# One core's decoder block: memory pools, instruction order and residual sums rearranged at four places

## Chip, cores and metric

One core of one Trainium2 chip. The metric is device microseconds of one execution; of several executions the median counts. The kernel before has run three times: 1854.45 us median, 1844.84 to 1854.69.

## The reference, cut to what matters

One layer of a decoder block on 512 tokens of width 1024, all in fp32. Every sub-block adds to the residual stream `x`:

```
x = x + hybrid_mixer(rmsnorm(x))            # DeltaNet and mLSTM heads, then mixed @ w_out
x = x + memory_cross_attention(rmsnorm(x), rmsnorm(mem))   # 256 memory tokens, 4 heads
x = x + peer_ffn(rmsnorm(x))                # 8 heads, each its 16 best of 128*128 experts
return rmsnorm(x)
```

In `peer_ffn` each token has per head two lists of 16 best keys; the sums of their values are the candidates, the 16 best candidates name the experts. With u and v the experts' rows of two tables of 16384 x 1024, the output of a token is the sum over its 128 experts of gate * gelu(u . h) * v.

## The kernel before

The 512 tokens are four tiles of 128. The mixer and cross attention work on the tiles in order. The experts are computed in two ways at once. Tiles 2 and 3 (DENSE, group G1) go over all experts: the dense loop (`peer_dense`) streams both tables in 128 blocks e of 128 experts, PE multiplies block e + 47 with the tokens ("pa", L1017), ACT applies Gelu (`act_`, L970), DVE multiplies by the gates, 8 blocks at a time (`gated`, L995; the gates come from DRAM through `gates_of` on POOL's queue), and PE adds block e to the outputs in PSUM (`add`, L998). In the last 47 blocks only `add` is left. Tiles 0 and 1 (G0) fetch the rows that each token needs: `peer_gather` issues from POOL one indirect DMA per expert slot (a "row": 128 tokens x 1024 values, 512 KB), 128 rows of u and then 128 rows of v for each tile, in the order u of tile 0, u of tile 1, v of tile 0, v of tile 1. DVE reduces a u row against the tokens (L1098) and accumulates a v row (L1109). Between them come Gelu on ACT (L1078) and the product with the gates (`weights_`). `close` adds the residual, loaded back from the output tensor, normalises, and stores.

`peer_gather` is a generator. A string, ORDER_XA, sets the order of cross attention and of what follows, and where rows are taken there ("p4" takes four): 158 of 512. In the dense loop 3.15 rows per block are taken, 2.3 in the last 47 blocks (L1035); what is left follows the loop (L1038). Then come the dense tiles' end (L1042 to L1065): residual and gains are loaded, the last block's products are added, DVE adds the residual out of PSUM into SBUF, ACT squares and sums, DVE scales, SP stores.

What is written is not the order in which an engine works. The framework orders each engine's instructions at build time, by the written order as priority and by its own estimate of when operands are ready; `keep_in_program_order` ties an instruction behind the one written before it on its engine. Each engine then takes its instructions strictly in order. Memory of a closed pool can be taken by a later pool, whose instructions wait until all instructions on the old pool's tiles are done.

At the seam between mixer and cross attention: the mixer's pools "mxp" and "mxw" hold its working tiles, and "mxp" also hT, the transposed activations, first of the input and then of the mixed heads. With hT the output projection is computed (`residual(..., "wout")`, L690 to L692; matmuls at L271, sums at L700), for tiles 0 and 1 first. When the mixer's `with` is left, pool "late" opens on the same memory. It holds all tiles of cross attention: gains (`row_(1, ...)`, L709, on POOL's queue), normalised tokens (W0), split weights (W2) and the transposed tokens of the two groups (dh0, dh1). `norm` (ACT squares, DVE scales, PE transposes at L209) and `query` (matmuls at L284) follow. Weights come through SP's queue into "w" and "wl", are copied to the leading part by ACT, and the rest is subtracted on POOL (L221) or DVE (L223).

`route_` of class Peer builds the candidates: per call seven additions on POOL (L844), on up to 8 heads x 16 values, then the 16 best on DVE. It is called five times (tile 0 in two halves), 35 additions.

Of the kernel before, what the change touches and what calls it, by code (L numbers as in the profile page):

```python
# [6 lines left out]
F32 = mybir.dt.float32  # L7
# [5 lines left out]
OP = mybir.AluOpType  # L13
# [62 lines left out]
def _body(ctx, tc, A, out, dbg):  # L76
# [137 lines left out]
    def hbuf(ph, n, name="hT"):  # L214
        t = ph.tile([P, 2, DB, n * P], F32R, name=name, bufs=1)
        return {"h": t[:, 0], "l": t[:, 1]}
# [380 lines left out]

    def mixer(tiles, aside):
        nt = len(tiles)
        with tc.tile_pool(name="mxp", bufs=nt) as ph, tc.tile_pool(name="mxw", bufs=2) as wk:  # L600
            ph = Phase(ph, tiles)
            hs = hbuf(ph, nt)
            mixed = {}
            steps = aside(wk)
            wr = wpool.tile([P, D], F32, name="wh")
# [78 lines left out]
            nc.sync.dma_start(x, A["x"].rearrange("(a p) d -> p a d", p=P))  # L684
            for ti in range(NT):
                X[ti] = x[:, ti]
            hs = hbuf(ph, nt)
            for i, ti in enumerate(tiles):
                transposed(mixed[ti].rearrange("p a b -> p (a b)"), hs, i)
            low_on[:] = [V]  # L690
            for k in range(0, nt, 2):
                residual(tiles[k:k + 2], {z: t[:, :, k * P:(k + 2) * P] for z, t in hs.items()}, "wout")  # L692
            for ti in tiles:
                tap(f"x1_{ti}", X[ti])

    def residual(tiles, hs, w):
        def ev(nb, i, ps):
            x = X[tiles[i]]
            c = slice(nb * 512, nb * 512 + 512)
            V.tensor_tensor(x[:, c], ps, x[:, c], op=OP.add)  # L700
        proj(hs, len(tiles), A[w], range(2), ev)
# [82 lines left out]
    class Peer:  # L784
# [50 lines left out]
        def route_(self, i, spot, hs, PH):  # L835
# [5 lines left out]
            off = 0  # L841
            for a0, n, w in RECT:
                o = cand[:, :, off:off + n * w].rearrange("p h (a b) -> p h a b", a=n)
                G.tensor_tensor(o, tvv[:, :, 0, a0:a0 + n].unsqueeze(3).to_broadcast([P, PH, n, w]),  # L844
                                tvv[:, :, 1, 0:w].unsqueeze(2).to_broadcast([P, PH, n, w]), op=OP.add)
                off += n * w
            yield
# [124 lines left out]
    def peer_dense(wu, psO, psC, rest):  # L972
# [40 lines left out]
        for e in range(NKEY):  # L1013
            n = e + AHEAD
            if n < NKEY:
                ps = psC.tile([P, 512], F32, name="pa")[:, :T]
                times(us.pop(0).rearrange("p (a b) -> p a b", a=DB), h, ps)  # L1017
            v = vs.pop(0)
            if e < NKEY - 1:
                for i in range(len(DENSE)):  # L1020
                    for z in range(2):
                        add(e, v, i, z)
            else:
                last.append((e, v))
            if n < NKEY:
                act_(n, ps)
            for g, at in gate_at.items():
                if at == e:
                    gated(g)
            for g, at in load_at.items():  # L1030
                if at == e:
                    gates_of(g)
            us.append(loaded_u(n + 2))
            vs.append(loaded_v(e + 2))
            steps += ROWS_BOTH if n < NKEY else ROWS_DOWN  # L1035
            run(rest, int(steps))
            steps -= int(steps)
        run(rest)  # L1038

        n = len(DENSE)  # L1040

# [7 lines left out]
        rs = []  # L1049
        for i, x in enumerate(xs):  # L1050
            for z, c in enumerate(half):
                for e, v in last:
                    add(e, v, i, z)
                V.tensor_tensor(x[:, c], outs[DENSE[i]][z], x[:, c], op=OP.add)
                SC.activation(junk[:, c], x[:, c], AF.Square, accum_out=ss[:, i, z:z + 1])
            if i:
                k = len(rs)
                t = sm.tile([P, n], F32, name="ft", bufs=1)
                V.tensor_tensor(t[:, k:i + 1], ss[:, k:i + 1, 0], ss[:, k:i + 1, 1], op=OP.add)
                r = rstd(t[:, k:i + 1], i + 1 - k, "n" if k == i else f"f{k}", 1.0 / D)  # L1060
                for j in range(k, i + 1):
                    rs.append(r[:, j - k:j - k + 1])
                    for c in half:
                        V.scalar_tensor_tensor(xs[j][:, c], xs[j][:, c], rs[j], w[:, c], op0=OP.mult, op1=OP.mult)
                        nc.sync.dma_start(out[DENSE[j] * P:(DENSE[j] + 1) * P, c], xs[j][:, c])  # L1065

    def peer_gather(ready, buffer):

        def fetch(table, ids, s):
            row = buffer()  # L1070
            G.indirect_dma_start(out=row, out_offset=None, in_=A[table],  # L1071
                                 in_offset=bass.IndirectOffsetOnAxis(ap=ids[:, s:s + 1], axis=0))
            return row
        late_, later = NSL // 2, NSL - 8

        def weights_(ti):

            SC.activation(act[ti], act[ti], AF.Gelu)  # L1078
            V.tensor_tensor(act[ti], act[ti], ready[ti], op=OP.mult)

        def close(ti):
            hn = first.hn[ti]
            x, wr, junk = buffer(), buffer(), buffer()
            G.dma_start(x, out[ti * P:(ti + 1) * P, :])
            row_(4, wr, G)
            V.tensor_tensor(hn, hn, x, op=OP.add)
            ss = sm.tile([P, 1], F32, name="nss")
            V.scalar_tensor_tensor(junk, hn, 1.0, hn, op0=OP.mult, op1=OP.mult, accum_out=ss)
            V.scalar_tensor_tensor(hn, hn, rstd(ss, 1, "n", 1.0 / D), wr, op0=OP.mult, op1=OP.mult)
            return out[ti * P:(ti + 1) * P, :], hn  # L1090

        act, done, stored = {}, [], []
        for ti in G0:
            act[ti] = per.tile([P, NSL], F32, name=f"act{ti}", bufs=1)
            hn, ids = first.hn[ti], first.ids[first.tiles.index(ti)].rearrange("p a b -> p (a b)")
# [7 lines left out]
        for ti in G0:  # L1103
            hn, ids = first.hn[ti], first.ids[first.tiles.index(ti)].rearrange("p a b -> p (a b)")
            for s in range(NSL):
                row = fetch("pv", ids, s)
                w = act[ti][:, s:s + 1]
                if s:
                    V.scalar_tensor_tensor(hn, row, w, hn, op0=OP.mult, op1=OP.add)  # L1109
                else:  # L1110
                    V.tensor_scalar(hn, row, w, None, op0=OP.mult)
                if s == later and ti == G0[0]:
                    weights_(done.pop())
                if s == late_ and ti != G0[0]:
                    stored.append(close(G0[0]))
                if s == late_ + 32 and stored:
                    G.dma_start(*stored.pop())
                yield
        G.dma_start(*close(G0[1]))

    mixer(tuple(range(NT)), memory_kv)
    mxs.close()
# [7 lines left out]

    def eight(t):
        return t[:, 0:2].rearrange("p a b -> p (a b)").rearrange("p (a b) -> p a b", a=DB)
    for i in range(2):
        t = late.tile([P, 2, DB, 2 * P], F32R, name=f"dh{i}")
        dh.append({"h": t[:, 0], "l": t[:, 1]})
    pe = ctx.enter_context(ExitStack())
    sct = pe.enter_context(tc.tile_pool(name="sct", bufs=1, side="right"))
# [57 lines left out]
    for what in ORDER_XA.split():  # L1195
# [3 lines left out]
        elif kind == "q":  # L1199
            n, x, y = (int(c) for c in what[1:])  # L1200
            query(GS[n], range(x, y))
            if n and y == DB:
                t = late.tile([P, 4, D], F32, name="dh1")
                dh[1] = {"f": eight(t), "room": t}
        elif kind == "s":
            soft_[n] = soft(n)
# [122 lines left out]
```

## Time and profile before

| | |
|---|---|
| median of three runs | 1854.45 us |
| profiled execution | 1853.35 us, span of its instructions 1851.6 us |
| busy PE / DVE / POOL / ACT | 90% / 69% / 45% / 22% of the span |
| moved by DMA | 519.02 MB, mean 280 GB/s |
| granted TensorE clock, mean | 0.957 of full speed |

The span runs from the first to the last instruction of the profiled execution; what lies around it is the difference to its time. Busy shares are averages over stages with different limits: up to about 490 us the mixer, to about 590 cross attention, then routing and gathers together, from about 1030 the dense loop beside the gathers, and from about 1820 the end. In a timeline a bracket names the idle time of the engine before the instruction and what ended it. PE's matmuls in fp32 stand as two records each.

### The profile page before, as it was taken

What the parts mean: (1) busy time and instruction counts of PE and PEld (TensorE: products, weight loads), DVE (VectorE), ACT (ScalarE), POOL (GpSimd) and SP (SyncE); (2) the same over time, 40 slices, a digit from 0 to 9 for tenths busy, and PEclk for the clock granted to TensorE, in tenths of its full rate; (3) what the DMA queues carried; (4) which work ended last, traced back from release to release, by engine and by line L of the source; (5) the groups of instructions that cost most, each with busy time, mean ns of one, the idle gap of its engine ahead of it and who ended that gap; (6) DMA issues with size and microseconds to landing.
All of it is one profiled execution on the core that took longest, in us unless ns stands there. A gap on an engine that the chain in (4) does not pass through costs nothing.

```text
span 1851.6 us, 21460 instructions
## 1 busy us (share of the span) xinstructions
PE 1671.7 (90%) x7468; PEld 1233.1 (67%) x7468; DVE 1269.1 (69%) x2789; ACT 406.2 (22%) x786; POOL 842.2 (45%) x685
## 2 busy tenths in 40 slices
PE   5999999999799976996999879993999999999993
PEld 3878788776598853885888656662666666664441
DVE  6656654665633698999998875557666566566668
ACT  5433532554353131211223110000000000000000
POOL 2121111331123054556354566566666666666663
PEclk9999999999899988998999979997999999999997
DMA  4211211235535477999899999999999999999996
GB/s 139 63 49 43 69 40 46 69 103 193 182 125 171 143 267 276 345 350 347 289 340 395 367 402 410 410 410 409 410 410 410 409 409 410 410 409 409 409 410 253
DMA packets 166508, 519.02 MB, mean 280 GB/s; under 512 B 15744, under 2 KB 44544, under 8 KB 164608
## 3 DMA queue, kind: packets, MB, share of 16 engines
q0 software_dynamic: 76752, 286.82, 39.6%
q1 hardware_dynamic: 60720, 216.15, 31.8%
q10 hardware_dynamic: 28928, 14.68, 2.7%
q8 instruction: 59, 0.97, 0.2%
q14 instruction: 49, 0.40, 0.1%
HBM read 498.71 MB, written 18.87 MB: 280 GB/s over the span
## 4 chain that ended last, share of the span: by engine, by line
DMA 36%; PE 33%; DVE 17%; issue 8%; POOL 4%; ACT 2%; ACTq 1%; SPq 0%; DVEq 0%; POOLq 0%
DMA row<-in_pv,ids 8%; PE pj L313 8%; PE pj L284 7%; PE pj L271 5%; PE acc L445 4%; DMA wh<-in_pv,ids 4%; DMA Vm<-in_pv,ids 3%; DMA W<-gates__132 3%; PE acc L943 3%; DMA W<-in_pv,ids 3%; DMA row<-in_pu,ids 3%; DMA wl<-in_pv,ids 2%; DVE W L1098 2%; DMA wl<-in_pu,ids 2%; DMA KT<-in_pu,ids 2%
## 5 line engine op out<-in xcount | busy, mean ns | idle before, releaser
L998 PE MATMUL o<-ld,W 128*128 128x512 f32 x832 | 371.3, 596 | 4.5 <-DVE W L951 4.5
L313 PE MATMUL pa<-dh,ld 128*128 128x256 f32 x1296 | 295.7, 381 | 35.8 <-ACT dh L970 34.2
L313 PEld LDWEIGHTS pa<-dh,ld 128*128 128x128 f32 x1296 | 247.4, 191 | 104.1 <-issue 39.3
L998 PEld LDWEIGHTS o<-ld,W 128*128 128x128 f32 x832 | 158.9, 191 | 175.9 <-issue 167.5
L221 POOL TENSOR_TENSOR wl<-w,wh 128x1024 fp32r<-128x1024 f32 x32 | 76.9, 2408 | 307.6 <-ACT wh L236 265.8
L313 PE MATMUL pj<-dh,w 128*128 128x256 f32 x640 | 148.0, 387 | 0.2 <-ACT dh L294 0.2
L1071 POOL DMA_INDIRECT W<-in_pu,ids x73 | 95.0, 1302 | 92.1 <-DVE W L1098 53.6
L313 PEld LDWEIGHTS pj<-dh,w 128*128 128x128 f32 x640 | 122.6, 195 | 17.2 <-ACT dh L294 0.7
L1109 DVE SCALAR_TENSOR_TENSOR dh<-row,act,dh 128x1024 f32<-128x1024 f32 x72 | 92.5, 1284 | 57.1 <-DMA row<-in_pv,ids 56.8
L1071 POOL DMA_INDIRECT row<-in_pu,ids x74 | 97.6, 1319 | 60.9 <-issue 19.3
L1071 POOL DMA_INDIRECT row<-in_pv,ids x74 | 99.4, 1343 | 51.3 <-issue 17.4
L970 ACT ACTIVATE W<-pa 128x256 f32<-128x256 f32 x65 | 24.9, 383 | 407.6 <-PE pa L313 397.5
L313 PE MATMUL pj<-dh 128*128 128x256 f32 x496 | 111.7, 379 | 0.0
L271 PE MATMUL pj<-wh,hT 128*128 128x512 f32 x320 | 108.5, 410 | 1.3 <-ACT wh L236 1.3
L284 PE MATMUL pj<-hT,wh 128*128 128x512 f32 x320 | 109.1, 414 | 0.0
L1098 DVE SCALAR_TENSOR_TENSOR row<-row,dh 128x1024 f32<-128x1024 f32 x74 | 88.4, 1222 | 22.5 <-DMA row<-in_pu,ids 22.1
L1098 DVE SCALAR_TENSOR_TENSOR W<-W,dh 128x1024 f32<-128x1024 f32 x73 | 88.5, 1220 | 19.2 <-DMA W<-in_pu,ids 19.2
L313 PEld LDWEIGHTS pj<-dh 128*128 128x128 f32 x496 | 93.5, 191 | 12.2
L236 ACT ACTIVATE wh<-w 128x1024 fp32r<-128x1024 f32 x64 | 67.7, 1058 | 106.8 <-DMA w<-in_wout 27.7
L998 PE MATMUL o<-ld,dh 128*128 128x512 f32 x192 | 85.2, 592 | 0.0
L1071 POOL DMA_INDIRECT wh<-in_pu,ids x40 | 56.6, 1415 | 51.2 <-DVE wh L1098 26.2
L1071 POOL DMA_INDIRECT wl<-in_pu,ids x41 | 54.6, 1332 | 47.8 <-PE pj L313 17.9
(432 smaller groups left out, 3143.5 us busy)
## 6 DMA issues: line engine op xcount, KB each, us to landing
ld<-in_pv SPq DMA_DIRECT2D x128, 512.0 KB, 6.8
ld<-in_pt SPq DMA_DIRECT2D x81, 512.0 KB, 6.9
gates__132<-W ACTq DMA_DIRECT2D x16, 896.0 KB, 16.4
W<-gates__132 POOLq DMA_DIRECT2D x14, 1024.0 KB, 17.4
w<-in_pt SPq DMA_DIRECT2D x24, 512.0 KB, 6.7
dh<-in_pt SPq DMA_DIRECT2D x23, 512.0 KB, 6.7
w<-in_win SPq DMA_DIRECT2D x20, 512.0 KB, 3.6
w<-in_wout SPq DMA_DIRECT2D x16, 512.0 KB, 3.7
```

The costliest lines, as they stand in the source:

```text
L221: G.tensor_tensor(out, a, hi, op=OP.subtract)
L236: SC.activation(hi, wt, AF.Copy)
L271: PE.matmul(acc[i], a[:, d, i * P:(i + 1) * P], b[:, z], start=d == 0 and m == 0, stop=d == DB - 1 and m == len(pairs) - 1)
L284: PE.matmul(acc[:, :n * P], a[:, d], b[:, d], start=d == 0 and m == 0, stop=d == DB - 1 and m == 2)
L313: PE.matmul(ps, w[:, d], h[:, d], start=d == 0, stop=d == DB - 1)
L445: PE.matmul(ps[:, i], l[:, i], r[:, i], start=True, stop=True)
L943: PE.matmul(ps[:, k], oj[:, a, :, k], og[:, g, a, :, k], start=g == 0, stop=g == 1)
L970: SC.activation(place(e), ps, AF.Gelu)
L998: PE.matmul(outs[DENSE[i]][z], place(e)[:, i * P:(i + 1) * P], v[:, z * 512:(z + 1) * 512], start=e == 0, stop=e == NKEY - 1)
L1071: G.indirect_dma_start(out=row, out_offset=None, in_=A[table], in_offset=bass.IndirectOffsetOnAxis(ap=ids[:, s:s + 1], axis=0))
L1098: V.scalar_tensor_tensor(row, row, 1.0, hn, op0=OP.mult, op1=OP.mult, accum_out=act[ti][:, s:s + 1])
L1109: V.scalar_tensor_tensor(hn, row, w, hn, op0=OP.mult, op1=OP.add)
```

## The change

- The mixer is cut in two. `mixed_tiles` does all up to the transposed mixed heads, with hT in a pool "mxh" of its own, and closes its working pools; `mixer` then computes the output projection. dh1 moves from "late" to a further pool "later".
- The candidates' additions go from POOL to VectorE.
- The Gelu on ACT between u and v rows is tied to its written place.
- Rows are counted (`taken`). The dense loop and the call behind it take all but the last 6 (TAIL) of 512; these follow the dense tiles' end, each tied to its written place on DVE, with the close of tile 1 and its store, which goes from POOL's queue to SP's.
- Dense tiles: PE adds the residual into PSUM by a product with the identity, and ACT and DVE read PSUM; DVE's four sums go. Gathered tiles: the residual is loaded with the first v row, which becomes a multiply-add on it, and the sum in `close` goes; the gains are loaded 8 rows ahead of `close`; scaling and store are done in halves.

```diff
     def mixer(tiles, aside):
         nt = len(tiles)
+        with tc.tile_pool(name="mxh", bufs=1) as hp:
+            hs = mixed_tiles(tiles, aside, hp)
+
+            low_on[:] = [V]
+            for k in range(0, nt, 2):
+                residual(tiles[k:k + 2], {z: t[:, :, k * P:(k + 2) * P] for z, t in hs.items()}, "wout")
...
+    def mixed_tiles(tiles, aside, hp):
+
+        nt = len(tiles)
         with tc.tile_pool(name="mxp", bufs=nt) as ph, tc.tile_pool(name="mxw", bufs=2) as wk:
             ph = Phase(ph, tiles)
-            hs = hbuf(ph, nt)
+            hs = hbuf(hp, nt)
...
-            hs = hbuf(ph, nt)
+            hs = hbuf(hp, nt)
             for i, ti in enumerate(tiles):
                 transposed(mixed[ti].rearrange("p a b -> p (a b)"), hs, i)
-            low_on[:] = [V]
-            for k in range(0, nt, 2):
-                residual(tiles[k:k + 2], {z: t[:, :, k * P:(k + 2) * P] for z, t in hs.items()}, "wout")
...
+            return hs
...
-                G.tensor_tensor(o, tvv[:, :, 0, a0:a0 + n].unsqueeze(3).to_broadcast([P, PH, n, w]),
+                V.tensor_tensor(o, tvv[:, :, 0, a0:a0 + n].unsqueeze(3).to_broadcast([P, PH, n, w]),
...
-            run(rest, int(steps))
+            run(rest, min(int(steps), 4 * NSL - TAIL - taken[0]))
             steps -= int(steps)
-        run(rest)
+        run(rest, 4 * NSL - TAIL - taken[0])
...
             for z, c in enumerate(half):
+                PE.matmul(outs[DENSE[i]][z], I, x[:, c], start=False, stop=False)
                 for e, v in last:
                     add(e, v, i, z)
-                V.tensor_tensor(x[:, c], outs[DENSE[i]][z], x[:, c], op=OP.add)
-                SC.activation(junk[:, c], x[:, c], AF.Square, accum_out=ss[:, i, z:z + 1])
+                SC.activation(junk[:, c], outs[DENSE[i]][z], AF.Square, accum_out=ss[:, i, z:z + 1])
...
-                    for c in half:
-                        V.scalar_tensor_tensor(xs[j][:, c], xs[j][:, c], rs[j], w[:, c], op0=OP.mult, op1=OP.mult)
+                    for z, c in enumerate(half):
+                        V.scalar_tensor_tensor(xs[j][:, c], outs[DENSE[j]][z], rs[j], w[:, c], op0=OP.mult, op1=OP.mult)
                         nc.sync.dma_start(out[DENSE[j] * P:(DENSE[j] + 1) * P, c], xs[j][:, c])
+        run(rest)
+        for to, half_ in stored:
+            nc.sync.dma_start(to, half_)
+
+    taken = [0]
+    TAIL = 6
+    stored = []
...
             row = buffer()
+            taken[0] += 1
...
-            SC.activation(act[ti], act[ti], AF.Gelu)
+            tc.keep_in_program_order(SC.activation(act[ti], act[ti], AF.Gelu))
...
-        def close(ti):
-            hn = first.hn[ti]
-            x, wr, junk = buffer(), buffer(), buffer()
+        def residual_(ti):
+            x = buffer()
             G.dma_start(x, out[ti * P:(ti + 1) * P, :])
-            row_(4, wr, G)
-            V.tensor_tensor(hn, hn, x, op=OP.add)
+            return x
+
+        def close(ti, wr):
+
+            hn, junk = first.hn[ti], buffer()
             ss = sm.tile([P, 1], F32, name="nss")
             V.scalar_tensor_tensor(junk, hn, 1.0, hn, op0=OP.mult, op1=OP.mult, accum_out=ss)
-            V.scalar_tensor_tensor(hn, hn, rstd(ss, 1, "n", 1.0 / D), wr, op0=OP.mult, op1=OP.mult)
-            return out[ti * P:(ti + 1) * P, :], hn
+            r = rstd(ss, 1, "n", 1.0 / D)
+            for c in (slice(0, 512), slice(512, D)):
+                V.scalar_tensor_tensor(hn[:, c], hn[:, c], r, wr[:, c], op0=OP.mult, op1=OP.mult)
+                stored.append((out[ti * P:(ti + 1) * P, c], hn[:, c]))
...
                 w = act[ti][:, s:s + 1]
-                if s:
-                    V.scalar_tensor_tensor(hn, row, w, hn, op0=OP.mult, op1=OP.add)
-                else:
-                    V.tensor_scalar(hn, row, w, None, op0=OP.mult)
+                done_ = V.scalar_tensor_tensor(hn, row, w, hn if s else residual_(ti), op0=OP.mult, op1=OP.add)
+                if taken[0] > 4 * NSL - TAIL:
+                    tc.keep_in_program_order(done_)
...
+                if s == late_ - 8 and ti != G0[0] or s == later and ti == G0[1]:
+                    wr = row_(4, buffer(), G)
                 if s == late_ and ti != G0[0]:
-                    stored.append(close(G0[0]))
+                    close(G0[0], wr)
                 if s == late_ + 32 and stored:
-                    G.dma_start(*stored.pop())
+                    for _ in range(2):
+                        G.dma_start(*stored.pop())
                 yield
-        G.dma_start(*close(G0[1]))
+        close(G0[1], wr)
...
+    lates = late, pool("later", 1, side="right")
     for i in range(2):
-        t = late.tile([P, 2, DB, 2 * P], F32R, name=f"dh{i}")
+        t = lates[i].tile([P, 2, DB, 2 * P], F32R, name=f"dh{i}")
```

## Rows read from the trace of the kernel before

**Rows 1.** Windows: stretch, length, busy PE, PEld, DVE, ACT, POOL, clock, DMA share, GB/s.

```profile
741.00:972.00 231.00, 215.58 (x1129) 191.28 (x1129) 224.81 (x703) 46.67 (x97) 124.32 (x98) 0.97 0.92 334
...
1111.00:1265.00 154.00, 154.00 (x534) 101.11 (x533) 89.84 (x137) 7.68 (x20) 95.71 (x70) 1.00 1.03 410
...
1265.00:1299.00 34.00, 0.08 (x1) 0.00 (x0) 29.38 (x46) 0.38 (x2) 24.32 (x24) 0.57 1.03 410
...
1825.00:1830.00 5.00, 0.00 (x0) 0.00 (x0) 4.86 (x5) 0.00 (x0) 0.00 (x0) 0.60 0.99 396
```

**Rows 2.** Timeline of PE, 487 to 503 us: start, duration, engine, line, what.

```profile
487.02 0.40 PE L271 MATMUL pj<-wh,hT 128*128 128x512 f32 x1
...
497.20 1.94 PE L209 MATMUL tr<-UI,W 128*128 128x128 f32 x8 [9.78 <-issue]
...
502.54 24.42 PE L284 MATMUL pj<-dh,W 128*128 128x256 f32 x192
```

**Rows 3.** Timeline of DVE, SP's queue and POOL around the same seam.

```profile
463.05 0.68 DVE L700 TENSOR_TENSOR x<-pj,x 128x512 f32<-128x512 f32 x1
...
482.00 2.89 SPq L246 DMA_DIRECT2D w<-in_wq  x2
...
487.74 0.74 POOL L191 DMA_DIRECT2D W<-in_nrow  x1 [59.46 <-PE pj L271]
...
490.68 2.34 POOL L221 TENSOR_TENSOR W<-w,W 128x1024 fp32r<-128x1024 f32 x1 [2.21 <-ACT W L251]
```

**Rows 4.** DMA issues, 480 to 500 us: count, KB each, us to landing.

```profile
w<-in_wq SPq DMA_DIRECT2D x4, 512.0 KB, 3.6
...
W<-in_nrow POOLq DMA_DIRECT2D x1, 512.0 KB, 8.1
```

**Rows 5.** Timeline of POOL and DVE, the candidates' additions and DVE's nearest operation.

```profile
673.64 1.17 POOL L844 TENSOR_TENSOR cand<-tv 128x32 f32<-128x32 f32 x6 [9.64 <-DVE tv L778]
...
838.09 0.23 DVE L859 TENSOR_TENSOR step<-key 128x120 f16<-128x120 f16 x1
...
838.22 0.21 DVE L781 MAX8 bv<-tk 128x8 f32<-128x50 f32 x1
...
838.25 6.80 POOL L844 TENSOR_TENSOR cand<-tv 128x128 f32<-128x128 f32 x7
...
869.24 1.23 DVE L1098 SCALAR_TENSOR_TENSOR row<-row,dh 128x1024 f32<-128x1024 f32 x1 [2.94 <-DMA row<-in_pu,ids]
```

**Rows 6.** Timeline of ACT and PE at the pause of 1265 us.

```profile
1298.62 0.31 ACT L1078 ACTIVATE act<-act 128x128 f32<-128x128 f32 x1 [50.33 <-DVE row L1098]
...
1299.26 5.91 PE L313 MATMUL pa<-dh,ld 128*128 128x256 f32 x16 [34.18 <-ACT dh L970]
```

**Rows 7.** Timeline of DVE and PE, the last 75 us.

```profile
1777.76 2.28 DVE L995 TENSOR_TENSOR dh<-dh,W 128x2048 f32<-128x2048 f32 x1
...
1793.55 27.63 PE L998 MATMUL o<-ld,dh 128*128 128x512 f32 x64
...
1808.42 1.28 DVE L1109 SCALAR_TENSOR_TENSOR dh<-row,act,dh 128x1024 f32<-128x1024 f32 x1 [0.32 <-DMA row<-in_pv,ids]
...
1833.51 1.22 DVE L1086 TENSOR_TENSOR dh<-dh,W 128x1024 f32<-128x1024 f32 x1
...
1834.77 1.22 DVE L1088 SCALAR_TENSOR_TENSOR KT<-dh 128x1024 f32<-128x1024 f32 x1
...
1836.04 0.15 DVE L174 TENSOR_SCALAR nv<-nss 128x1 f32<-128x1 f32 x1
...
1838.36 1.28 DVE L1089 SCALAR_TENSOR_TENSOR dh<-dh,nr,W 128x1024 f32<-128x1024 f32 x1
...
1839.56 2.48 DVE L1054 TENSOR_TENSOR ld<-o,ld 128x512 f32<-128x512 f32 x4
...
1842.91 0.16 DVE L1059 TENSOR_TENSOR ft<-fss 128x2 f32<-128x2 f32 x1 [0.88 <-ACT ld L1055]
...
1845.49 2.74 DVE L1064 SCALAR_TENSOR_TENSOR ld<-ld,f0r 128x512 f32<-128x512 f32 x4
```

More of the change, by code (lines that the diff above doesn't have):

```diff
@@ L599, in mixer @@
         nt = len(tiles)
+        with tc.tile_pool(name="mxh", bufs=1) as hp:
[3 more added lines that the diff above has]
+                residual(tiles[k:k + 2], {z: t[:, :, k * P:(k + 2) * P] for z, t in hs.items()}, "wout")
+            for ti in tiles:
+                tap(f"x1_{ti}", X[ti])
+    def mixed_tiles(tiles, aside, hp):
+        nt = len(tiles)
         with tc.tile_pool(name="mxp", bufs=nt) as ph, tc.tile_pool(name="mxw", bufs=2) as wk:
             ph = Phase(ph, tiles)
-            hs = hbuf(ph, nt)
+            hs = hbuf(hp, nt)
             mixed = {}
@@ L686, in mixer @@
                 X[ti] = x[:, ti]
-            hs = hbuf(ph, nt)
+            hs = hbuf(hp, nt)
             for i, ti in enumerate(tiles):
                 transposed(mixed[ti].rearrange("p a b -> p (a b)"), hs, i)
-            low_on[:] = [V]
-            for k in range(0, nt, 2):
-                residual(tiles[k:k + 2], {z: t[:, :, k * P:(k + 2) * P] for z, t in hs.items()}, "wout")
-            for ti in tiles:
-                tap(f"x1_{ti}", X[ti])
+            return hs
     def residual(tiles, hs, w):
@@ L1076, in weights_ @@
         def weights_(ti):
-            SC.activation(act[ti], act[ti], AF.Gelu)
+            tc.keep_in_program_order(SC.activation(act[ti], act[ti], AF.Gelu))
             V.tensor_tensor(act[ti], act[ti], ready[ti], op=OP.mult)
-        def close(ti):
-            hn = first.hn[ti]
-            x, wr, junk = buffer(), buffer(), buffer()
+        def residual_(ti):
+            x = buffer()
             G.dma_start(x, out[ti * P:(ti + 1) * P, :])
-            row_(4, wr, G)
-            V.tensor_tensor(hn, hn, x, op=OP.add)
+            return x
+        def close(ti, wr):
+            hn, junk = first.hn[ti], buffer()
             ss = sm.tile([P, 1], F32, name="nss")
             V.scalar_tensor_tensor(junk, hn, 1.0, hn, op0=OP.mult, op1=OP.mult, accum_out=ss)
-            V.scalar_tensor_tensor(hn, hn, rstd(ss, 1, "n", 1.0 / D), wr, op0=OP.mult, op1=OP.mult)
-            return out[ti * P:(ti + 1) * P, :], hn
-        act, done, stored = {}, [], []
+            r = rstd(ss, 1, "n", 1.0 / D)
+            for c in (slice(0, 512), slice(512, D)):
+                V.scalar_tensor_tensor(hn[:, c], hn[:, c], r, wr[:, c], op0=OP.mult, op1=OP.mult)
+                stored.append((out[ti * P:(ti + 1) * P, c], hn[:, c]))
+        act, done = {}, []
         for ti in G0:
@@ L1202, in _body @@
             if n and y == DB:
-                t = late.tile([P, 4, D], F32, name="dh1")
+                t = lates[1].tile([P, 4, D], F32, name="dh1")
                 dh[1] = {"f": eight(t), "room": t}
```

## The prediction, made before the changed kernel ran

> **What bounds the kernel now.** I read the windows by stage first, then the PE timeline at the seam between mixer and cross attention, then the waits, then the DVE timeline of the last 45 us. The windows [rows 1] show three regimes. From 741 to 972 us DVE is busy 224.8 of 231 us while the DMA engines move 334 GB/s: DVE sets the pace. From 1111 us on the DMA share is 1.03 and the rate stands at 410 GB/s, in the stretch where PE works all the time (1111 to 1265) and also in the one where PE does nothing (1265 to 1299); at 1825 it is still 396. So from 1111 at the latest to about 1827 the gathered rows and the streamed tables together fill the DMA engines, and PE is not what ends the stage. Behind that comes a tail on DVE alone. Ahead of all of it, at 487 us, PE stands still while memory changes hands [rows 2, 3].
>
> The profiled execution took 1853.35 us and its span 1851.6, so 1.75 us lie around the span. It is 1.1 us below the median of the three runs, 1854.45 (1844.84 to 1854.69). A difference of 0.5%, 9.3 us, is about what a measurement of this kernel can tell from none.
>
> **1. Cross attention beside the mixer's last product.** Now the last matmul of the output projection ends at 487.4 and the first query matmul starts at 502.54 [rows 2]. Between them lie the load of the norm's gains on POOL (L709), which waited for the last matmul, POOL standing for 59.46 us, and then landed after 8.1 us [rows 3, 4], the two norms, and 16 transposes. POOL waited since all tiles of pool "late" wait for the mixer's pool, which holds hT, the operand of that product. Afterwards hT lives in a pool of its own, and only "later" (dh1, which the second pair of tiles needs) shares its memory: the gains, the norm of tiles 0 and 1 and their transposes can run from 463.7, when these tiles' sums are finished [rows 3], beside PE's second half of the product. What then holds the queries? The weights' buffers come from the old rotation: the first load issues at 482.00 and lands 3.6 us later, at 485.6; copy and subtraction (2.21 and 2.34) put the last part at 490.2 at the latest, and the first two of three passes need less [rows 3, 4]. The transposes stay on PE, now inside the product: 16 cost at most 3.9 at the 1.94 for 8 of [rows 2], nothing where they fall into PE's waits for weights; I take 2, and the product ends at 489.4. The 512 KB of gains then load beside the product's weights: at most 1.3 us at 410 GB/s. So queries start near 490.5: **-12 us**. From there to about 650 PE is the chain, so all later work moves along. Ends: 0 (the seam stays) and -15.1 (the whole gap).
>
> **2. Candidates' sums on DVE.** 35 additions leave POOL, where they stand in front of gathers; the last seven held it 6.8 us [rows 5]. On DVE the nearest row, 120 elements of two inputs, lasts 0.23 and the next one starts 0.13 later: 35 of them are 4.6 to 8.1 us. DVE is full there, so this lies on the path; I take 4.9, since most of these tiles have 24 to 64 columns. Against it stands the 2.94 us that DVE waited at 869 for a row, whose issue stood behind those 6.8 us. Sum **+2 us**; ends +8.1 (nothing saved) and -7.7 (the 9.64 us for which POOL stood at the second seven come back as well). The Trainium skill, "Perfetto Trace Analysis", Identifying the Most-Contended Engine, says to relieve the engine with the highest occupancy, which speaks against this part. By it the whole 4.9 us would be lost and the sum be 1845.5; the trace agrees as to the engine, with 224.8 of 231 us.
>
> **3. The pinned Gelu.** ACT's Gelu of the second gathered tile's activations (L1078) stands too early in ACT's order: it waited 50.33 us for that tile's last product, the evictions of "pa" stood behind it, and PE stood 34.18 us [rows 6]. Pinned to its program place it comes at row 376 of 512; 158 rows are taken in the written order and 3.15 per block of the dense loop, so that is e = 69, and the products it waits for are 120 rows old. It waits for nothing. PE gets 34 us ahead. I cost this at nothing: while PE stood, the DMA engines moved 410 GB/s of gathered rows, and those rows are now moved later instead. The Trainium skill, "Perfetto Trace Analysis", Optimization Strategies, says to free what blocks the matmul engine when it idles; by that rule the 34 us come off. The trace disagrees as far as the rate goes. What is late next: gated(15) (L995) stands behind row 479 in DVE's order (33 rows follow it) and was done at 1780.0, 13.5 us before PE used its tiles at 1793.55 [rows 7]; with PE 34 us ahead PE waits there. A row is 512 KB, 1.28 us at 410 GB/s. At worst 27 rows (34.18 / 1.28) are consumed without streamed tables beside them, at DVE's 1.32: **+1.1 us**; ends 0 and 1.1.
>
> **4. The tail.** From 1808.42 DVE has 19 rows at 1.32 to 1833.51; then the residual 1.26, square 1.27, rstd 2.32, scaling 1.2, four sums 2.5, a wait of 0.88 for ACT, rstd 2.58, four scalings to 1848.23 [rows 7]: 39.8 us. Afterwards: the residual load and the gains come at rows 385 and 504, ahead of rows that they now delay by 2 x 1.28, so I count 21 rows, 27.7; dense rstd 2.6 and scalings 2.7 between rows 506 and 507; square 1.3, rstd 2.3, two half scalings 1.4: 38.0. That is **-1.8 us**; the last store lands as before. PE gets four identity matmuls, each two records of 0.43: 3.4 us, so PE ends at 1824.6 and ACT 0.8 later. DVE would arrive after row 506, at 1828, so this is covered by 2.6 us. If that cover is gone, DVE waits with six rows and the closing behind it. The first row of each tile becomes a multiply-add like the others and one 1.22 addition of the first tile goes, both under the DMA limit. On SP the last two half stores stand behind the four dense ones; on POOL the two residual loads and two gains' loads move ahead of gathers, at about the 0.74 of such a load in [rows 3], and the first tile's store becomes two: under 4 us of issue in a stage of some 700 that waits for the transfers.
>
> Sum: 1853.35 - 12 + 2 + 1.1 - 1.8 = **1842.6 us**, 0.64% below the median.
>
> **Rivals.** (a) PE's stall is the bound. The 34.18 us would come off too, and the 1.1 of part 3 with them: 1842.6 - 35.3 = 1807.3. For it: PE works without a pause around the stall [rows 1]. Against it: 410 GB/s through the stall. The rule of the Trainium skill that part 3 names leads here. 7%.
>
> (b) The gathers between 650 and 1080, where DVE's order is redrawn by the scheduler, fill the idle DMA time better: at 334 of 410 GB/s over 231 us there are 43 us of transfers to be had; a quarter gives 1832. 8%.
>
> (c) The overlap does not come: the norm waits for the seam after all, or the gain is lost before 1080. Then 1853.35 + 2 + 1.1 - 1.8 = 1854.6. For it: the order on each engine is the scheduler's, which may put the norms behind the product. Against it: nothing else held POOL at the seam than the product [rows 3]. 15%.
>
> (d) Slower: the six pinned rows wait for PE. Place: DVE's first instruction of the dense end. Behind gated(15) PE needs 2.3 + 27.6 + 3.4 and ACT 0.8, 34 us; DVE gets from row 479 to 506 in 35.6. From row 481 on, each row that gated(15) slips back costs 1.3 us; from row 497 on the change is slower; behind row 505 DVE waits 32 us with everything queued: 1842.6 + 32 = 1875. Against it: the Gelu at e = 69 holds back the scheduler's picture of the rows, which draws gated(15) forward. 8%.
>
> **How the numbers follow.** The forecast has 62%, with 1832 to 1852 as its own range (overlap -15 to -8, sums -4 to +8, order). Faster by over 0.5% means below 1845.2: 0.45 of the forecast's 0.62, (a) and (b): 0.60. Slower, above 1863.7: most of (d) and a little of (c): 0.08. The rest 0.32. The range 1826 to 1860 leaves out (a), most of (d) and the edges.
>
> **What would show it.** Right: the first query matmul near 490, the gains' load on POOL issued near 442 with no wait for the last product; no Gelu wait on ACT and no PE gap at 1265; the DMA rate at 410 GB/s until some 38 us before the end; 35 additions of 0.13 to 0.23 on DVE; and between rows 506 and 507 no wait. Wrong: a span that falls with the PE gap, a seam that stays, or a wait of DVE for ACT ahead of the dense scaling.

## The result, and the profile after

The changed kernel takes 1842.06 us (median of 15 runs, 1837.02 to 1845.13); the kernel before, run beside it, takes 1850.37 us (15 runs, 1844.83 to 1859.73). The ratio is 0.9946, with an interval of 0.9932 to 0.9960: by it 10.0 us (7.4 to 12.6) of 1850.4 are gone, by the two medians 8.3. The prediction of 1842.6 us holds in its value, and of its range, 1826 to 1860, little was needed. Three of its parts came out at about their size; the fourth, the candidates, cost 2.8 us alone and 3.7 to 5.9 in pairs of kernels, where +2 was put.

The profiled execution of the changed kernel took 1837.1 us (span 1835.3), 5 us less than its median; that of before took 1853.35 (span 1851.6), 3 more than its new median. So the two traces differ by 16.3 us where the medians differ by 8.3, and sizes of a few us are read from rounds of runs here, not from two traces.

First the windows, which answer [rows 1] (stretch, length, busy PE, PEld, DVE, ACT, POOL with counts, granted clock, DMA share, GB/s), of the changed kernel:

```profile
741.00:972.00 231.00, 222.69 (x1173) 197.69 (x1172) 222.10 (x697) 51.83 (x103) 114.59 (x82) 0.98 0.95 344
1111.00:1265.00 154.00, 154.00 (x539) 102.16 (x538) 89.07 (x140) 9.03 (x24) 93.99 (x72) 1.00 1.03 410
1265.00:1299.00 34.00, 34.00 (x121) 22.61 (x120) 20.15 (x30) 1.90 (x5) 19.50 (x17) 1.00 1.03 410
```

From 1265 to 1299 us PE is now busy for all 34.00 us, where it had been busy for 0.08; the DMA engines move 410 GB/s in both. The regimes are the same: VectorE full to about 972, the DMA engines full from 1111 at the latest.

Where the time went shows in the bytes. The same view over longer stretches, first of the kernel before:

```profile
0.00:460.00 460.00, 418.66 (x2332) 337.82 (x2333) 274.84 (x723) 207.53 (x379) 95.75 (x57) 0.98 0.25 81
460.00:650.00 190.00, 177.15 (x1012) 156.01 (x1011) 96.38 (x333) 71.44 (x123) 34.12 (x70) 0.96 0.48 155
650.00:1100.00 450.00, 388.90 (x1928) 320.17 (x1927) 408.63 (x1227) 95.22 (x199) 240.79 (x201) 0.92 0.92 337
...
1250.00:1700.00 450.00, 415.82 (x1395) 266.00 (x1394) 289.00 (x255) 20.78 (x55) 293.76 (x224) 0.96 1.03 410
```

and of the changed kernel:

```profile
0.00:460.00 460.00, 420.75 (x2349) 339.96 (x2350) 277.69 (x729) 210.09 (x383) 96.55 (x58) 0.99 0.26 83
460.00:650.00 190.00, 180.39 (x1041) 159.09 (x1041) 107.53 (x389) 71.30 (x131) 43.48 (x71) 0.99 0.54 177
650.00:1100.00 450.00, 401.30 (x1947) 328.20 (x1948) 407.49 (x1211) 94.19 (x190) 228.33 (x170) 0.93 0.94 340
...
1250.00:1700.00 450.00, 450.00 (x1456) 276.45 (x1455) 275.43 (x236) 20.17 (x53) 285.56 (x213) 1.00 1.03 410
```

Length times rate gives the megabytes. Up to 460 us the changed kernel is 0.9 MB ahead (38.2 against 37.3), from 460 to 650 it gains 4.2 (33.6 against 29.5), from 650 to 1100 another 1.4 (153.0 against 151.7). Together that is 6.4 MB, and at 410 GB/s 15.7 us: nearly the whole 16.3 us between the spans. The 0.9 MB ahead of the seam are scatter and not the change: by 460 us the fourteen traces of this document, those of the experiments among them, have moved 37.2 to 38.3 MB, with the old seam as with the new one. From 460 to 650 us the ten kernels with the new seam move 31.6 to 34.3 MB and the four with the old one 29.4 to 30.3, on the mean 3.2 MB apart, or 7.8 us. From 650 to 1100 the two kinds do not differ (150.1 to 153.1 and 149.8 to 154.5). After 1250 both move 410 GB/s, though PE works 34 us more in that stretch than before.

At the seam itself, which answers [rows 2, 3], the timeline of PE and POOL in the changed kernel:

```profile
436.61 0.74 POOL L191 DMA_DIRECT2D W<-in_nrow  x1 [12.90 <-PE tr L209]
...
464.83 0.71 PE L209 MATMUL tr<-UI,W 128*128 128x128 f32 x5
...
483.52 0.39 PE L271 MATMUL pj<-wh,hT 128*128 128x512 f32 x1
483.75 0.71 PE L209 MATMUL tr<-UI,W 128*128 128x128 f32 x5
485.20 0.38 PE L284 MATMUL pj<-dh,W 128*128 128x256 f32 x1 [0.74 <-ACT dh L211]
485.93 3.25 PE L284 MATMUL pj<-dh,W 128*128 128x256 f32 x25 [0.34 <-DVE dh L212]
491.06 20.17 PE L284 MATMUL pj<-dh,W 128*128 128x256 f32 x166 [1.88 <-DVE W L223]
```

The gains load at 436.6 with no wait for the last product. Eleven of the 16 transposes run inside the product from 464.8 on, the last five behind it, and the queries start at 485.20, where they had started at 502.54. What holds them next is the low part of the weights, 1.88 us, after which the other 166 records run on from 491.06.

The end, which answers [rows 7], from the timeline of DVE:

```profile
1712.67 2.28 DVE L1003 TENSOR_TENSOR dh<-dh,W 128x2048 f32<-128x2048 f32 x1
...
1812.46 1.28 DVE L1128 SCALAR_TENSOR_TENSOR dh<-row,act,dh 128x1024 f32<-128x1024 f32 x1 [0.85 <-DMA row<-in_pv,ids]
1813.66 0.15 DVE L1067 TENSOR_TENSOR ft<-fss 128x2 f32<-128x2 f32 x1
...
1816.63 2.73 DVE L1072 SCALAR_TENSOR_TENSOR ld<-o,f0r,ld 128x512 f32<-128x512 f32 x4 [0.32 <-DVE f0r L183]
1819.27 1.28 DVE L1128 SCALAR_TENSOR_TENSOR dh<-wh,act,dh 128x1024 f32<-128x1024 f32 x1
...
1827.18 1.22 DVE L1106 SCALAR_TENSOR_TENSOR KT<-dh 128x1024 f32<-128x1024 f32 x1
...
1830.77 1.41 DVE L1109 SCALAR_TENSOR_TENSOR dh<-dh,nr,row 128x512 f32<-128x512 f32 x2
```

The dense end stands between rows 506 and 507; its only wait is 0.32 us, for a result of VectorE itself. PE's last product, by its timeline, ends here:

```profile
1738.78 24.20 PE L1006 MATMUL o<-ld,dh 128*128 128x512 f32 x56
...
1768.82 1.02 PE L1006 MATMUL o<-ld,dh 128*128 128x512 f32 x2
```

At 1769.8, 51.4 us earlier than before (1821.2). The rows go on behind it at VectorE's pace of 1.32 us, for 44 us to the dense end and then the last six. The DMA engines move 408 to 413 GB/s there up to 1800, 35 us before the end.

### The profile page after: what moved, and what is told of

Read it like the earlier page. It is cut to its first block, busy times and chain, and to the rows that moved or that the text cites. A ratio compares the mean times of both kernels' runs of the same rounds, so it can differ in the third digit from the quotient of the medians.

```text
span 1835.3 us, 21469 instructions
## 1 busy us (share of the span) xinstructions
PE 1672.3 (91%) x7476; PEld 1233.9 (67%) x7476; DVE 1267.4 (69%) x2820; ACT 406.8 (22%) x786; POOL 826.7 (45%) x650
## 4 chain that ended last, share of the span: by engine, by line
DMA 38%; PE 32%; DVE 18%; issue 5%; POOL 4%; ACT 2%; ACTq 1%; SPq 0%; DVEq 0%; POOLq 0%
PE pj L284 8%; PE pj L313 7%; PE pj L271 6%; DMA wh<-in_pv,ids 5%; DMA KT<-in_pv,ids 4%; DMA row<-in_pv,ids 4%; DMA row<-in_pu,ids 4%; PE acc L445 4%; DMA wl<-in_pv,ids 3%; DMA Vm<-in_pv,ids 3%; PE acc L951 2%; DMA gates__132<-W 2%; DVE W L1118 2%; DMA W<-in_pu,ids 2%; DMA W<-in_pv,ids 2%
## 5 line engine op out<-in xcount | busy, mean ns | idle before, releaser
L313 PEld LDWEIGHTS pj<-dh,w 128*128 128x128 f32 x640 | 123.9, 196 | 17.9 <-ACT dh L294 0.7
L1118 DVE SCALAR_TENSOR_TENSOR W<-W,dh 128x1024 f32<-128x1024 f32 x73 | 88.1, 1219 | 16.7 <-DMA W<-in_pu,ids 15.1
```

What stands on the lines that cost most here:

```text
L313: PE.matmul(ps, w[:, d], h[:, d], start=d == 0, stop=d == DB - 1)
L1118: V.scalar_tensor_tensor(row, row, 1.0, hn, op0=OP.mult, op1=OP.mult, accum_out=act[ti][:, s:s + 1])
```

## The experiments

The twelve further kernels form three groups, each beside runs of the kernel before, whose medians were 1851.72 us (the four parts alone), 1854.33 (gains later, the same with the candidates on GpSimd, Gelu not pinned, no rows held back) and 1850.06 (the other four). The ratios are to these, so compare ratios, and not medians, between groups. The last two columns are worked out: the bytes that were moved by 1250 us (added up from windows of 10 us), and what the span has left when 1250 us and the rest of the 519 MB at 410 GB/s are taken off.

| kernel | median us (runs) | ratio to before, interval | MB by 1250 us | left over, us |
|---|---|---|---|---|
| before | 1850.37 (15) | | 279.9 | 18.4 |
| changed | 1842.06 (15) | 0.9946, 0.9932 to 0.9960 | 286.5 | 18.2 |
| overlap alone | 1840.26 (6) | 0.9941, 0.9929 to 0.9953 | 286.6 | 18.3 |
| candidates alone | 1853.24 (12) | 1.0015, 1.0002 to 1.0029 | 280.2 | 17.8 |
| Gelu alone | 1852.77 (12) | 0.9997, 0.9981 to 1.0012 | 284.6 | 18.4 |
| tail alone | 1850.45 (12) | 0.9987, 0.9974 to 0.9999 | 278.9 | 15.7 |
| changed, gains later | 1845.48 (10) | 0.9945, 0.9928 to 0.9962 | 282.4 | 16.8 |
| the same, candidates on GpSimd | 1839.25 (6) | 0.9917, 0.9889 to 0.9944 | 283.4 | 15.8 |
| changed, Gelu not pinned | 1843.35 (7) | 0.9945, 0.9926 to 0.9965 | 283.8 | 15.2 |
| changed, no rows held back | 1869.16 (6) | 1.0080, 1.0059 to 1.0102 | 282.6 | 42.1 |
| the same, last stores on POOL | 1842.68 (8) | 0.9953, 0.9934 to 0.9973 | 284.2 | 21.4 |
| changed, candidates on GpSimd | 1834.74 (6) | 0.9914, 0.9893 to 0.9935 | 283.7 | 15.4 |
| overlap and tail | 1835.40 (6) | 0.9925, 0.9899 to 0.9951 | 286.7 | 17.9 |
| overlap and tail, gains later | 1838.27 (6) | 0.9940, 0.9918 to 0.9962 | 285.6 | 17.1 |

Both derived columns belong to the one profiled execution, which need not be a typical one (that of "changed, candidates on GpSimd", 1841.02 us, was the slowest of its six). They carry the main finding: while the bytes by 1250 us differ by 7.8 MB (19 us), the time left over stays within 15.2 to 18.4 us in all kernels but the two with no rows held back. PE's last product ends between 1769.8 and 1826.8 us in these, and the time left over does not follow it: 15.4 with an early end at 1774.7, 18.3 with a late one at 1811.1.

### The four parts alone

**Overlap alone.**

```diff
-            hs = hbuf(ph, nt)
+            hs = hbuf(hp, nt)
...
-        t = late.tile([P, 2, DB, 2 * P], F32R, name=f"dh{i}")
+        t = lates[i].tile([P, 2, DB, 2 * P], F32R, name=f"dh{i}")
```

> The kernel before with the overlap alone (hT in a pool of its own, dh1 in the pool behind it). Theory, the overlap carries the gain: the first query matmul near 485 us instead of 502.5, and the lead is kept to the end, -12 us (-8 to -15) against the kernel before, ratio 0.992 to 0.996. Rival, the gain comes from the other parts or is lost before 1100 us: the seam closes the same way, and the time stays within 2 us of before.

0.9941 of 1851.7 is 10.9 us less (8.7 to 13.1), the whole gain of the change. PE's timeline at the seam of this kernel:

```profile
484.11 0.40 PE L271 MATMUL pj<-wh,hT 128*128 128x512 f32 x1
...
485.79 0.38 PE L284 MATMUL pj<-dh,W 128*128 128x256 f32 x1 [0.74 <-ACT dh L211]
```

and, for the old seam, of the Gelu alone:

```profile
481.08 0.39 PE L271 MATMUL pj<-wh,hT 128*128 128x512 f32 x1
...
496.58 24.41 PE L284 MATMUL pj<-dh,W 128*128 128x256 f32 x192
```

From the end of the product to the first query it is 1.3 us here and in all ten kernels with the new seam, and 15.0 to 15.6 us in all four with the old one (487.42 to 502.54 before). Where the product itself ends scatters from trace to trace, from 481.5 to 491.0, so the start of the queries by itself, from 485.0 to 492.3 with the new seam and 496.6 to 502.5 with the old, does not give the gain. What is gained at the seam is 15.1 less 1.3 less the two waits behind the first queries (0.34 and 1.88): 11.6 us, less what the eleven transposes cost inside the product. The pause of PE is still there, 37.6 us in this kernel, and does not keep it from having the changed kernel's time. The rival falls.

**Candidates alone.**

```diff
-                G.tensor_tensor(o, tvv[:, :, 0, a0:a0 + n].unsqueeze(3).to_broadcast([P, PH, n, w]),
+                V.tensor_tensor(o, tvv[:, :, 0, a0:a0 + n].unsqueeze(3).to_broadcast([P, PH, n, w]),
```

> The kernel before with the 35 sums of the candidates on VectorE alone. Theory of the prediction: +2 us, between +5 (the additions all lie on VectorE's path and no wait of VectorE falls) and -3 (VectorE's waits for gathers fall by more). Rival: the gathers that no longer stand behind the sums fill the DMA engines between 650 and 1000 us, and the lead shows in the bytes moved by 1000 us: -5 us or more.

+2.8 us (0.4 to 5.4). The 35 additions, by their line in the changed kernel (duration in ns, shortest, median and longest, and the commonest forms):

```profile
L852 DVE TENSOR_TENSOR cand<-tv x35: 161/189/293, 618.8 to 830.6; 128x64 f32<-128x64 f32 x8, 128x32 f32<-128x32 f32 x7, 128x24 f32<-128x24 f32 x5, 128x128 f32<-128x128 f32 x3
```

Added up singly their records give some 6.9 us, but they overlap: VectorE is busy with them for 5.56 us in this experiment's trace, by its window from 600 to 1100 us, and for 5.54 in the changed kernel's. VectorE's waits from 600 to 1100 us (waiting line, releaser: us in total, times, longest), of the kernel before:

```profile
...
DVE W L1098 <- DMA W<-in_pu,ids: 10.3, 5, 6.2
DVE row L1098 <- DMA row<-in_pu,ids: 5.8, 3, 2.9
DVE Vm L932 <- PE acc L943: 5.5, 4, 1.9
DVE wh L1098 <- DMA wh<-in_pu,ids: 5.3, 3, 2.6
DVE W L995 <- DMA W<-gates__132: 4.9, 1, 4.9
```

and of candidates alone:

```profile
...
DVE W L995 <- DMA W<-gates__132: 9.5, 1, 9.5
DVE Vm L932 <- PE acc L943: 9.3, 4, 6.4
DVE wh L1098 <- DMA wh<-in_pu,ids: 4.7, 3, 3.5
DVE W L1098 <- DMA W<-in_pu,ids: 4.7, 1, 4.7
...
DVE row L1098 <- DMA row<-in_pu,ids: 3.6, 2, 3.1
```

The waits for gathered rows do fall, from 21.4 us on these lines to 13.0. But those for the gates rise by 4.6, and the ones for PE on these lines by 3.8, in the same execution; all waits that the view lists add up to 67.0 us before and 67.5 here. What the gathers give back is waited for elsewhere, as far as one trace of each shows. By 1000 us, where the rival looked, 183.3 MB are moved against 179.7 before, but the Gelu alone and the tail alone, which lack this part, have moved 183.8 and 183.2 by then, and by 1250 us it is 280.2 against 279.9: the rival's lead is not there.

**Gelu alone.**

```diff
-            SC.activation(act[ti], act[ti], AF.Gelu)
+            tc.keep_in_program_order(SC.activation(act[ti], act[ti], AF.Gelu))
```

> The kernel before with the second Gelu kept at its program place alone. Theory, the DMA engines bound this stage: PE loses its 34 us gap at 1265 us and ends some 34 us earlier, 1787 instead of 1821, and the time stays within +-2 us, as the bytes are the same and they flow at 410 GB/s in both. Rival, PE's stall is on the path: -34 us, 1816. A halfway case, the stall lets the gathered rows run ahead and their lead is lost at the end, where VectorE takes 1.32 us a row against 1.28 of the DMA engines: +1 to +2.

The window that answers [rows 1] of this kernel, in which PE has no pause any more:

```profile
1265.00:1299.00 34.00, 34.00 (x121) 22.61 (x120) 20.18 (x32) 1.92 (x5) 20.78 (x16) 1.00 1.03 410
```

PE ends at 1772.9 instead of 1821.2, and the time is that of before, 0.9997. A gain of 34 us would have been a ratio of 0.982; the interval ends at 0.9981.

**Tail alone** (all of `peer_dense` and `peer_gather` in the diff but the Gelu).

```diff
+                PE.matmul(outs[DENSE[i]][z], I, x[:, c], start=False, stop=False)
...
-        run(rest)
+        run(rest, 4 * NSL - TAIL - taken[0])
```

> The kernel before with the tail alone (six rows behind the dense tiles' end, residuals in the sums, scaling in halves, gains loaded early; the Gelu where it was). Theory of the prediction: 38.0 us instead of 39.8 behind PE's last row of loads, -1.8 us. Theory after the changed kernel's trace: the tail is 3 to 4 us shorter, but the gains of the first closing, loaded 8 rows early, hold a row's buffer, a gather stands for 9.6 us at the head of POOL's queue near 1725 us and the DMA engines move 1.7 MB less there, so -2 to +2. Rival: no such stand without the pinned Gelu, and -4.

-2.4 us (0.2 to 4.8). The stand of a gather for 9.65 us at the head of POOL's queue is there without the pinned Gelu too, released at 1725.38, so the rival's reason falls; its -4 lies in the interval, as do -1.8 and -2. Here PE ends about as late as the prediction had it (1826.8, for 1824.6), and the cover can be read from DVE and ACT:

```profile
1828.58 1.29 DVE L1120 SCALAR_TENSOR_TENSOR dh<-row,act,dh 128x1024 f32<-128x1024 f32 x1 [0.77 <-DMA row<-in_pv,ids]
1829.78 0.15 DVE L1059 TENSOR_TENSOR ft<-fss 128x2 f32<-128x2 f32 x1
```

```profile
1827.40 0.19 ACT L1055 ACTIVATION_READ_ACCUMULATOR ld<-o 128x1 f32 x1
```

ACT's last sum is ready at 1827.6, VectorE comes to the dense end at 1829.78: 2.2 us of cover.

### The closing, the pinned Gelu and the rows held back

**Gains later.** In the changed kernel POOL's timeline at the first tile's closing, and the window around it:

```profile
1722.43 1.43 POOL L1087 DMA_INDIRECT W<-in_pv,ids  x1 [1.03 <-DVE row L1106]
1733.50 0.94 POOL L1087 DMA_INDIRECT wh<-in_pv,ids  x1 [9.64 <-DVE nt L181]
1734.74 0.93 POOL L1087 DMA_INDIRECT W<-in_pv,ids  x1 [0.30 <-issue]
```

```profile
1720.00:1750.00 30.00, 30.00 (x72) 13.26 (x71) 22.28 (x31) 0.00 (x0) 15.88 (x14) 1.00 0.94 352
```

Of two "wh" rows one holds the gains from 1691 to 1737 us, and the gathers behind the waiting one stand as well. 30 us at 352 instead of 410 GB/s are 1.7 MB, or 4.2 us.

```diff
-                if s == late_ - 8 and ti != G0[0] or s == later and ti == G0[1]:
+                if s == late_ - 1 and ti != G0[0] or s == later and ti == G0[1]:
```

> The changed kernel with the gains of the first closing loaded one row ahead of it instead of eight (POOL's queue meets them at row 63 of the second sums, not 56). Theory, the gains that hold a row's buffer from 1691 to 1737 us make a gather stand 9.6 us at the head of POOL's queue, and the DMA engines lose 1.7 MB there: that stand falls below 3 us, the rate stays at 405 to 410 GB/s between 1700 and 1760, and -2 to -4 us against the changed kernel (1838 to 1840, ratio to the kernel before 0.993). Rival, VectorE, which takes 1.32 us a row for the last 75 us, ends the stage whatever the gathers do there: the stand goes and the time stays within 1 us of the changed kernel's 1842.

The longest stand at the closing falls to 4.6 us (below 3 was expected) and the dip is gone from its place, with 409 GB/s from 1720 to 1740 and 401 to 1760. But from 1760 to 1780 the rate is 372, where the changed kernel has 412, and the ratio stays: 0.9945 after 0.9946. No gain of 2 to 4 us is seen, as the rival had it, and the same edit without the other two parts gives nothing either:

> The same with the gains of the first closing loaded one row ahead of it. Theory: the dip of the DMA engines at the closing shrinks by some 0.5 to 1 MB, -1 to -2 us against y1. Rival, as in x1: no change beyond 1 us.

0.9940 against 0.9925 of the kernel that it was made from, with intervals that overlap. The stand is real and has no price that these runs resolve.

**Candidates back on GpSimd, in two places** (the one line above turned back).

> The same, with the candidates' 35 sums back on GpSimd. Theory, part 2 costs: 35 additions of 6.9 us in sum on a full VectorE, of which the part alone gave +2.8 us: -2 to -4 us against x1, 1835 to 1837. Rival, with the overlap in place the gathers behind the sums matter more: +2 us against x1.

> The changed kernel with the candidates' 35 sums back on GpSimd. Theory, the sums cost +2 to +3 us on a full VectorE, in the changed kernel as alone: -2 to -3 us, ratio to the kernel before 0.992 to 0.9935. Rival, they cost nothing here: the ratio stays at 0.9946.

0.9917 against 0.9945, and 0.9914 against 0.9946: 5.2 and 5.9 us less. A third pair differs by the same line: overlap and tail, 0.9925, and the changed kernel with the Gelu not pinned, 0.9945, 3.7 us. The intervals overlap in the first and third pair and just meet in the second, but all three and the part alone have the same sign. 5.2 and 5.9 lie beyond the 2 to 4 and the 2 to 3 expected, by less than the runs resolve. The changed kernel with this one line turned back has the lowest ratio of all.

**Gelu not pinned.**

```diff
-            tc.keep_in_program_order(SC.activation(act[ti], act[ti], AF.Gelu))
+            SC.activation(act[ti], act[ti], AF.Gelu)
```

> The changed kernel with the second Gelu not pinned. Theory, DMA bound: the PE gap of 34 to 38 us is back at about 1255 us, PE ends near 1806 instead of 1770, the gated product of the last group stands behind row 478 instead of 442, and the time stays within +-2 us of the changed kernel. Rival 1, PE's stall is on the path: +30 us or more. Rival 2, the six pinned rows wait for PE, as its end comes close to VectorE's row 506 (1814 us): VectorE waits ahead of the dense scaling, +2 to +8 us.

PE's longest wait in this kernel after 1112 us:

```profile
PE pa L313 <- ACT dh L978: 37.1, 1, 37.1
```

PE ends at 1814.7 (expected 1806), VectorE waits only 0.3 us ahead of the dense scaling, and the ratio is 0.9945 after 0.9946. So the pause costs nothing that can be seen in the changed kernel either, and the six rows have room even then (ACT is done at 1815.5, the dense end starts at 1817.3).

**No rows held back.**

```diff
-    TAIL = 6
+    TAIL = 0
```

> The changed kernel with no rows held back (0 instead of 6): the dense tiles' end stands behind the closing of the second tile in VectorE's order. Theory of the prediction: the 5.7 us of the dense end no longer lie beside the landing of the last six rows, VectorE waits for the last rows instead, +2 to +5 us. Rival, VectorE is the bound of the last 75 us and does the same work in any order: within +-1 us.

+25 us against the changed kernel: neither theory. The timeline of SP's queue and of VectorE shows why:

```profile
1828.98 1.01 SPq L1076 DMA_DIRECT2D out<-dh  x2
1830.08 2.62 SPq L985 DMA_DIRECT2D ld<-in_pv  x5
...
1833.56 1.26 SPq L985 DMA_DIRECT2D ld<-out  x2
...
1859.89 0.16 DVE L1067 TENSOR_TENSOR ft<-fss 128x2 f32<-128x2 f32 x1 [30.27 <-ACT ld L1063]
```

The last two half stores, which the change had moved from POOL's queue to SP's, stand here in front of the last five loads of the table. They wait for VectorE's closing, the loads wait for them, PE waits 79.5 us for the loads, and VectorE 30.27 for what comes of them. With the stores back on POOL's queue:

```diff
         for to, half_ in stored:
-            nc.sync.dma_start(to, half_)
+            G.dma_start(to, half_)
```

> No rows held back, and the last two half stores of the second tile on POOL's queue instead of SP's. Theory, the +25 us of the kernel with no rows held back came from SP's queue alone: there the two stores stood in front of the last five table loads and waited for VectorE's closing at 1828 us. With the stores on POOL the loads flow early, PE ends near 1770, and the time is within +-3 us of the changed kernel, 1839 to 1846. Rival, the order on VectorE is what costs (the dense end behind the closing): +5 us or more against the changed kernel, with VectorE waiting for ACT or PE ahead of the dense sums.

0.9953: the 25 us are gone, PE ends at 1773.4, and holding six rows back is worth at most a few us by itself. The time left over, 21.4 us against 18.2, hints at 3; the ratios, 0.9953 and 0.9946, do not resolve it.

**Overlap and tail.** The kernel before with these two parts.

> The kernel before with the overlap and the tail, the candidates on GpSimd and the Gelu not pinned. Theory: the sum of the two parts alone, -10.9 and -2.4, so -13 us against the kernel before (ratio 0.9928, 0.991 to 0.9945), and the stretch behind the last of the bytes is 15 to 16 us instead of 18, as PE's gap costs nothing and the later PE end leaves fewer rows at VectorE's pace. Rival, the parts do not add up: no faster than the changed kernel.

0.9925, 13.9 us less than before (9.1 to 18.7), as the sum of the two. The time left over is 17.9, not the 15 to 16 expected; single traces scatter by that much.

## Why the prediction was right, and where it was not

**The whole.** The four parts alone give -10.9, +2.8, -0.6 and -2.4: together -11.1, and the change measures -10.0. The parts add up within their intervals, some 2 to 3 us each. That the value is met within 0.5 us is luck in part: the sum starts from the profiled execution, 1853.35, which lay 3.0 us above the median of the kernel before, 1850.37. From that median the same terms give 1839.7, 2.4 us below what was measured; the errors of the terms and of the start cancel.

**Part 1, the overlap (-12).** Right in mechanism and size: -10.9 alone (8.7 to 13.1 less). The gains load early, the transposes go into the product, and the weights' low part is what holds the queries next, as worked out. In detail the seam went otherwise. The queries do not start as late as 490.5: the first 26 matmul records start 1.3 us behind the product, and the low part then costs 1.88 us in between. The prediction took the 2.21 of [rows 3] for the copy; it is POOL's idle time, and the copy on ACT lasts 1.06 in the changed kernel. The low part comes from VectorE there, at 491.01, 0.8 us behind the 490.2 "at the latest". The product ended at 483.9 in this trace and not at 489.4; the change cannot be read from that, since its end scatters by 9.5 us over the traces. The whole gap, -15.1, was not to be had, since 1.3 us of it and 2.2 us of waits remain. That the gain keeps to the end is the second half of the step: 4.2 MB of lead arise between 460 and 650 us, and from 1250 to 1700 both kernels move 410 GB/s, so that it is kept.

**Part 2, the candidates (+2).** The sign was right, and +2 lies in the interval of the part alone (0.4 to 5.4), but all four measurements are higher: 2.8 alone, 3.7, 5.2 and 5.9 in the pairs. The term that was mis-sized is less "I take 4.9", for which the traces show 5.56 us, than the "2.94 us that DVE waited" set against it: in the trace of the part alone VectorE's waits as a whole do not fall (67.0 and 67.5 us). The Trainium skill, "Perfetto Trace Analysis", Identifying the Most-Contended Engine, says to optimise the engine with the highest occupancy first. The prediction had read from it that the whole 4.9 would be lost; the pairs lie nearer to that than to +2, the part alone does not, and the runs do not decide between the two.

**Part 3, the Gelu (0 to +1.1).** Right, and this is the step that mattered: -0.6 us alone with an interval of -3.5 to +2.2, and nothing when it is turned back. Rival (a), 1807.3, falls. The Trainium skill, "Perfetto Trace Analysis", Optimization Strategies, says to keep the matmul engine going by optimising the engines that block the critical path when it idles. Here a pause of 34 to 37 us of PE was not on that path: of four pairs of kernels with and without the pinned Gelu (before and Gelu alone; Gelu not pinned and changed; overlap and tail and changed with the candidates on GpSimd; these two with gains later) none differs by more than 4.3 us, with intervals that overlap. One step in it was wrong: "with PE 34 us ahead PE waits there", at gated(15). That product stood not behind row 479 but behind row 442 in VectorE's order, was done at 1715.0 (1712.67 and 2.28), and PE came to it at 1738.78. The pinned Gelu is what moved it: it stands behind row 441 or 442 in all seven kernels with that part and behind 478 or 479 in all seven without. The prediction had the reason in hand, as evidence against its rival (d), that the Gelu draws gated(15) forward, and did not use it in the step itself. So PE did not wait there and ended 51 us earlier. What the step put a price on came out near its count: from 1753.17 on 51 rows come at VectorE's 1.32, almost without a wait, where it had been 19 from 1808.42 on. That is 32 more instead of 27, and 32 times 0.04 is 1.3 us, less than the runs resolve.

**Part 4, the tail (-1.8).** Right in size, -2.4 alone. Not seen were two things in it. "under 4 us of issue" on POOL left out that the gains keep a row's buffer, with the 9.64 us stand; no price of it shows here. And "On SP the last two half stores stand behind the four dense ones" was taken as a small matter of order, while 25 us hang on where these stores stand, as the run with no rows held back shows. The cover was put at 2.6 us; it is 2.2 in the tail alone, and 44 us in the changed kernel (1813.66 less 1769.8), where PE is early.

**The other rivals.** (b), gathers that fill the DMA engines from 650 to 1080: 1.4 MB in the two traces, 3.4 us, not the 11 that a quarter would be, and no difference over all fourteen (149.8 to 154.5 MB from 650 to 1100 us with the old seam, 150.1 to 153.1 with the new). (c), no overlap: fell at the seam. (d), the held rows behind PE: nothing of it in the changed kernel, where gated(15) went the other way; a loss of nearly that size, 25 of its 32 us, came with no rows held back, but from SP's queue.

## What to carry to other kernels

Add up the bytes moved by a given time. Where the rate stands flat at its ceiling to near the end, what puts bytes ahead of that stretch counts, and a pause of another engine inside it can be free: PE's 34 to 37 us were, as long as PE still ended ahead of the place where VectorE needs its result. Compare a seam by the distance between the work before and behind it, since the work before it scatters too. When a store moves to another queue, look at which loads stand behind it there: here two stores that waited for VectorE's last instruction held five loads back, and that cost 25 us. And small work moved onto a full engine is not paid by the waits that it was to remove: those fell here, and others rose by as much.

## What the runs showed of the hardware that was not expected

The DMA engines moved 410 GB/s over 450 us with PE busy for 415.82 or 450.00 of them, and after 1250 us twelve of fourteen kernels ended within 3.2 us of each other once their bytes are counted. That points to the time ahead of 1250 us as the place where executions come to differ: the profiled execution of the Gelu alone took 1841.95 us, 10.8 less than the median of that kernel, and had moved 4.7 MB more by 1250 us than that of before, or 11.5 us at 410 GB/s. No two executions of one kernel were traced, so this is shown only between kernels.
